# A Conformer convolution module: VectorE's tap sums in PSUM, five taps of each block on TensorE, a layer norm in a written-out order

## The chip, the cores and the metric

One Trainium2 chip, one of its cores. The metric is the device time of one execution in microseconds; lower is better. Engines by the names of the profile: PE is TensorE's matrix products (PEld its weight loads), DVE is VectorE, ACT is ScalarE, POOL is GpSimd, SP issues the DMAs.

## The reference, cut to what matters

An encoder of two layers on 256 tokens of 2048 features, in float32. The first layer's mixer is the convolution module, the second's is a gated DeltaNet; each is followed by a SwiGLU feed-forward. Only the convolution module is touched.

```python
def conformer_conv_module(h, w_pw1, b_pw1, w_dw, b_dw, ln_g, ln_b, w_pw2, b_pw2):
    u = h @ w_pw1 + b_pw1                      # 2048 -> 4096
    a, gate = jnp.split(u, 2, axis=-1)
    u = a * jax.nn.sigmoid(gate)
    u = depthwise_conv_centred(u, w_dw) + b_dw  # 31 taps along the tokens, per feature
    u = jax.nn.silu(layernorm(u, ln_g, ln_b))   # over the 2048 features of a token
    return u @ w_pw2 + b_pw2                    # 2048 -> 2048
```

## The kernel before

Activations lie with features on the 128 partitions and the 256 tokens along the free dimension, in 16 blocks of 128 features. A product is made block by block of output features (`products`): 512 KB chunks of float32 weights (`raw`, three buffers) are loaded by SP, ACT rounds half a chunk (128 x 512) to a high part `hi` (line 159), DVE subtracts to get the low part `lo` (line 160), and PE adds hi x hi, hi x lo and lo x hi in PSUM (lines 189 to 191, or 184 and 185 in the wide form). There are four buffers each for `hi` and `lo`, so these splits run at most 48 products ahead of PE.

The convolution module loops over the 16 feature blocks j. Each block has two products (`pa` and `pg`, 48 matmuls each), DVE scales them by the token's factor `rstd` (`ta`, line 325, `tg`, line 328), ACT makes the sigmoid, DVE joins them into `u` (line 330), which lies in a zero-padded tile `up`. The 31 taps of the depthwise convolution are shifted views of `up`, and they are divided among the engines:

- ACT makes tap 0 with the bias into `a` (line 336).
- For blocks 12 to 15 PE makes 8, 8, 16 and 16 taps as products with diagonal matrices (line 340), which POOL builds at the start (line 290, 48 of them).
- POOL adds 15 taps (14, 13, 6 and 5 for the last four blocks) to `a` (line 344), from products `m` that ACT makes with four buffers (line 343).
- DVE makes the rest in two running sums `b[0]` and `b[1]` in SBUF (lines 350, 352, 354); the sums are added to `a` by POOL (line 355), DVE (line 358), and for PE's part DVE (line 357).

For the layer norm, sums over the channels are made by PE with a matrix of ones (`s1` of the deviations from the first four blocks' mean `shift`, `s2` of their squares, line 302). From block 6 on the shift is subtracted within the taps (line 350), for the earlier ones by POOL (line 308). After block 15 come `dm`, `dq`, `var`, the square root on ACT and the reciprocal on DVE, and then 16 blocks of normalising: multiply by `lr` (line 386; three on DVE, thirteen on POOL), subtract `dm` (line 389, DVE), SiLU (ACT), and the split into `y` hi and lo (lines 203, 204). Then the second product `pw2` starts with three column blocks at once, all of whose `hi` and `lo` have six buffers.

Each engine's queue is in order. The order in it is set at build time by a planner, which sorts by the order of the code and by priorities (`high_priority`). The six column halves of `pw2` that fit are split before the layer norm. Four lines of the program:

```python
                w = lambda t: wdw[:, j * TAPS + t : j * TAPS + t + 1]
                x = lambda t: up[:, t : t + S]
                acc, b = new(f"a{j}", 1), (new("b0", 2), new("b1", 2))
                npe, npool = NPE.get(j, 0), NPOOL[j]
```

Of the kernel before, what the change touches and what calls it, by code (L numbers as in the profile page):

```python
# [7 lines left out]
F32 = mybir.dt.float32  # L8
# [17 lines left out]
# PSUM banks  # L26
# [3 lines left out]
LNP = 100  # L30
FIRST = 4
SHIFTED = 6
NPE = {12: 8, 13: 8, 14: 16, 15: 16}
# [4 lines left out]
# taps of the depthwise convolution that GpSimd adds, by feature block  # L38
NPOOL = [15] * 12 + [14, 13, 6, 5]

# columns of the packed per-feature parameters
# [11 lines left out]
# columns of the packed constants  # L53
# [13 lines left out]
def fv(ap, off, *dims):  # L67
    """A view of a tile by an offset and [stride, count] pairs over its free elements."""
    return bass.AP(ap.tensor, ap.offset + off, [list(ap.ap[0]), *[list(d) for d in dims]])


class Trunk:
# [20 lines left out]
    def new_h(self):  # L93
        """The residual stream on chip, in a pool of its own."""
        self.hs = ExitStack()
        hp = self.hs.enter_context(self.tc.tile_pool(name=self.nm("resid"), bufs=1))
        self.h = [hp.tile([P, S], F32, tag=f"h{k}", name=self.nm(f"h{k}")) for k in range(KD)]
# [5 lines left out]
    def load_first(self, srcs):  # L103
        """The input and the first weights, in the order in which they are needed."""
# [47 lines left out]
    def halves(self, raw, i, n, pool=None):  # L152
        """k-tiles i to i + n as a high and a low part that float32r holds exactly."""
# [9 lines left out]
    def products(self, srcs, kt, acts, wide=False, tags=("lin",), pool=None, order=None):  # L163
        """Blocks of 128 output features, k-tile by k-tile; acts: float32r tiles [P, hi | lo].

        order: of the k-tiles, within each CS of them."""
# [77 lines left out]
    def warm(self, func, after):  # L244
        """Loads a function's table on ScalarE, ahead of its use."""
# [3 lines left out]
    def rsqrt(self, src, scale, eps, then=None):  # L249
# [5 lines left out]
        nc.vector.reciprocal(r, r)  # L255
        return r

    def norm_end(self):
        """The factor is traced behind the next product, whose result is the first to need it."""
# [4 lines left out]

    def conv_module(self, next_norm):
# [3 lines left out]
        with tc.tile_pool(name="conv", bufs=1, reuse_waits="tile") as cv:  # L269
# [16 lines left out]
            diag = {}  # L286
            for j, n in NPE.items():
                for t in range(1, 1 + n):
                    g = cv.tile([P, P], F32, name=f"diag{j}_{t}")
                    nc.gpsimd.tensor_scalar(g, self.mat("ident"), wdw[:, j * TAPS + t : j * TAPS + t + 1], 0.0,  # L290
                                            op0=ALU.mult, op1=ALU.add)
                    diag[j, t] = g
# [4 lines left out]
            def add(key, t, n, last):  # L297
                """Sums over the channels, added up in PSUM."""
                if n == 0:
                    tag = "a" if key == "s1" else "b"  # L300
                    sums[key] = self.ps.tile([P, S], F32, tag=tag, bufs=PSB[tag], name=self.nm(key))
                nc.tensor.matmul(sums[key], self.mat("ones"), t, start=(n == 0), stop=last)

            def second(j):
                """The deviation from the first channels' mean, and its square's sum."""
# [6 lines left out]
                nc.scalar.activation(sq, d, AF.Square)  # L312
# [3 lines left out]
            for j in range(KD):  # L316
# [11 lines left out]
                nc.vector.tensor_tensor(tg, pg, rstd, op=ALU.mult)  # L328
                nc.scalar.activation(tg, tg, AF.Sigmoid, bias=self.p("bpw1", KD + j))
                nc.vector.scalar_tensor_tensor(u, ta, self.p("bpw1", j), tg, op0=ALU.add, op1=ALU.mult)  # L330

                w = lambda t: wdw[:, j * TAPS + t : j * TAPS + t + 1]
                x = lambda t: up[:, t : t + S]
                acc, b = new(f"a{j}", 1), (new("b0", 2), new("b1", 2))
                npe, npool = NPE.get(j, 0), NPOOL[j]
                nc.scalar.activation(acc, x(0), AF.Identity, scale=w(0), bias=self.p("bdw", j))
                if npe:
                    pt = self.ps.tile([P, S], F32, tag="b", bufs=PSB["b"], name=self.nm("taps"))
                    for t in range(1, 1 + npe):
                        nc.tensor.matmul(pt, diag[j, t], x(t), start=(t == 1), stop=(t == npe))  # L340
                for t in range(1 + npe, 1 + npe + npool):
                    m = new("m", 4)
                    nc.scalar.activation(m, x(t), AF.Copy, scale=w(t))  # L343
                    nc.gpsimd.tensor_tensor(acc, acc, m, op=ALU.add)  # L344
                t0 = 1 + npe + npool
                for t in range(t0, TAPS):
                    k = t - t0
                    r = b[k % 2]
                    if k == 1 and j >= SHIFTED:
                        nc.vector.scalar_tensor_tensor(r, x(t), w(t), shift, op0=ALU.mult, op1=ALU.subtract)  # L350
                    elif k < 2:
                        nc.vector.tensor_scalar(r, x(t), w(t), None, op0=ALU.mult)
                    else:
                        nc.vector.scalar_tensor_tensor(r, x(t), w(t), r, op0=ALU.mult, op1=ALU.add)
                (nc.vector if j == KD - 1 else nc.gpsimd).tensor_tensor(acc, acc, b[0], op=ALU.add)
                if npe:
                    nc.vector.tensor_tensor(b[1], b[1], pt, op=ALU.add)
                nc.vector.tensor_tensor(acc, acc, b[1], op=ALU.add)
# [13 lines left out]
            # mean = shift + dm: the first channels' deviations add up to nothing  # L372
# [5 lines left out]
            nc.vector.scalar_tensor_tensor(var, sums["s2"], 1.0 / D, dq, op0=ALU.mult, op1=ALU.subtract)  # L378
            lr = self.rsqrt(var, 1.0, self.c("eps5"), AF.Silu)
            # in the order in which VectorE and GpSimd get them done  # L380
            order = (0, 3, 1, 2, *range(4, KD))
            ys = [None] * KD
            for n, j in enumerate(order):
                d = ds[j]
                with tc.high_priority(LNP * (KD - n)):
                    (nc.vector if j < 3 else nc.gpsimd).tensor_tensor(d, d, lr, op=ALU.mult)
                    if j == 0:
                        nc.vector.tensor_tensor(dm, dm, lr, op=ALU.mult)
                    nc.vector.tensor_tensor(d, d, dm, op=ALU.subtract)
                    nc.scalar.activation(d, d, AF.Silu, scale=self.p("lng", j), bias=self.p("lnb", j))  # L390
                    y = cv.tile([P, 2 * S], F32R, tag=f"y{j}", name=self.nm("y"))
                    self.split(y, d)
                ys[j] = y
            self.norm_begin()
            first = self.products(self.pw2[:3], KD, ys, wide=True, tags=("lin", "lin", "g"), pool=cv, order=order)
# [44 lines left out]

    def deltanet(self, next_norm):
# [8 lines left out]
        # what the last heads leave early lies below what they need to the end  # L450
# [25 lines left out]
        # the first lie within what dn0 leaves  # L476
# [17 lines left out]
    # tiles of the DeltaNet's pool: shape, number  # L494
# [34 lines left out]
    def dn_gates(self):  # L529
        """ln(beta) and the decays' sums within a block: as a token's scalars and along the tokens."""  # L530
# [9 lines left out]
        # ln(1 + e) = 2 artanh(e / (2 + e))  # L540
# [42 lines left out]
    def short_conv(self, n):  # L583
        """Twice the SiLU of the five-tap convolution, of feature block n."""
# [92 lines left out]
    def dn_lanes(self, xd):  # L677
        """Inverses of the 32 x 32 diagonal blocks of I + X, one block in a partition."""
# [29 lines left out]
        # pairs of 4, 8 and 16  # L708
# [56 lines left out]
        # pairs of 32  # L765
# [191 lines left out]
```

## Time and profile before

| | |
|---|---|
| median of 3 runs | 3095.36 us (3088.73 to 3097.14) |
| span of the profiled execution | 3092.0 us |
| that execution's time against the median | no separate time of it is on the page; its span lies 3.4 us, or 0.1%, under the median of the runs |
| DVE, PE, POOL busy in the whole span | 2332.2, 2859.3 and 1009.9 us |
| first and last `u` of the convolution module | start 32.6 and 319.2 us |
| first product of the layer-normed data | 347.7 us |
| third column block of `pw2` complete | 364.2 us |

Busy times are unions of the instructions on an engine; an instruction's duration is longer than the distance to the next one, since neighbours overlap by some 70 ns on DVE. In rows of groups the columns are the line, the engine, the operation, output and inputs, count, then the busy time and the mean of one in ns, and then the idle time just before them with what ended it.

### The profile page before, as it was taken

What the parts mean: (1) busy time and instruction counts of PE and PEld (TensorE: products, weight loads), DVE (VectorE), ACT (ScalarE), POOL (GpSimd) and SP (SyncE); (2) the same over time, 40 slices, a digit from 0 to 9 for tenths busy, and PEclk for the clock granted to TensorE, in tenths of its full rate; (3) what the DMA queues carried; (4) which work ended last, traced back from release to release, by engine and by line L of the source; (5) the groups of instructions that cost most, each with busy time, mean ns of one, the idle gap of its engine ahead of it and who ended that gap; (6) DMA issues with size and microseconds to landing.
All of it is one profiled execution on the core that took longest, in us unless ns stands there. A gap on an engine that the chain in (4) does not pass through costs nothing. (4 is left out here: it accounts for less than half of the span.)

```text
span 3092.0 us, 50294 instructions
## 1 busy us (share of the span) xinstructions
PE 2859.3 (92%) x18122; PEld 2566.7 (83%) x18122; DVE 2332.2 (75%) x3735; ACT 1695.6 (55%) x3449; POOL 1009.9 (33%) x1047
## 2 busy tenths in 40 slices
PE   7778799999999999878888889888999999999998
PEld 6777688888888889877888888888888888888887
DVE  8999876666666667899899997985766666666555
ACT  6665555555555445654665456554545555555443
POOL 6777420000000111566667766562110000000111
PEclk9999899999999999999999999999999999999999
DMA  4333266555556665543544445456666555556664
GB/s 164 121 112 103 89 202 189 188 185 188 186 186 193 197 200 166 181 150 115 164 155 149 137 144 166 129 158 200 192 189 209 185 187 188 185 187 184 192 190 141
DMA packets 163866, 521.38 MB, mean 169 GB/s; under 512 B 18240, under 2 KB 34944, under 8 KB 163616
## 3 DMA queue, kind: packets, MB, share of 16 engines
q1 hardware_dynamic: 162320, 516.86, 52.7%
q8 instruction: 142, 2.33, 0.3%
q10 hardware_dynamic: 1296, 1.30, 0.1%
q14 instruction: 108, 0.88, 0.1%
HBM read 497.02 MB, written 21.07 MB: 168 GB/s over the span
## 5 line engine op out<-in xcount | busy, mean ns | idle before, releaser
L160 DVE TENSOR_TENSOR lo<-raw,hi 128x512 fp32r<-128x512 f32 x1764 | 1384.7, 788 | 644.6 <-ACT hi L159 638.3
L159 ACT CAST hi<-raw 128x512 fp32r<-128x512 f32 x1764 | 1085.9, 619 | 935.4 <-PE acc L185 692.8
L185 PE MATMUL acc<-xs,hi 128*128 128x512 f32 x2816 | 982.0, 398 | 0.6 <-ACT hi L159 0.6
L184 PE MATMUL acc<-xs,lo 128*128 128x256 f32 x2640 | 742.3, 281 | 0.0
L191 PE MATMUL acc<-xs,lo 128*128 128x256 f32 x2064 | 620.1, 302 | 96.4 <-DVE lo L160 95.6
L189 PE MATMUL acc<-xs,hi 128*128 128x256 f32 x2064 | 606.1, 295 | 31.1 <-ACT hi L159 18.9
L185 PEld LDWEIGHTS acc<-xs,hi 128*128 128x128 f32 x2816 | 517.7, 188 | 116.4 <-ACT hi L159 0.9
L190 PE MATMUL acc<-xs,hi 128*128 128x256 f32 x2064 | 605.2, 294 | 0.8 <-DVE xs L220 0.7
L191 PEld LDWEIGHTS acc<-xs,lo 128*128 128x128 f32 x2064 | 410.9, 200 | 128.8 <-DVE lo L160 123.0
L184 PEld LDWEIGHTS acc<-xs,lo 128*128 128x128 f32 x2640 | 499.0, 189 | 6.8
L185 PE MATMUL acc<-hs,hi 128*128 128x512 f32 x1408 | 486.8, 391 | 0.0
L189 PEld LDWEIGHTS acc<-xs,hi 128*128 128x128 f32 x2064 | 413.8, 201 | 37.1 <-ACT hi L159 21.1
L190 PEld LDWEIGHTS acc<-xs,hi 128*128 128x128 f32 x2064 | 413.9, 201 | 6.1 <-issue 4.3
L184 PE MATMUL acc<-hs,lo 128*128 128x256 f32 x1376 | 388.0, 282 | 0.0
L421 POOL TENSOR_TENSOR tg<-tg,rstd 128x256 f32<-128x256 f32 x88 | 65.0, 738 | 920.9 <-ACT tg L420 920.9
L185 PEld LDWEIGHTS acc<-hs,hi 128*128 128x128 f32 x1408 | 262.2, 188 | 53.4
L184 PEld LDWEIGHTS acc<-hs,lo 128*128 128x128 f32 x1376 | 259.9, 189 | 1.6
L230 POOL TENSOR_TENSOR sq<-h 128x256 f32<-128x256 f32 x59 | 55.0, 931 | 562.7 <-DVE h L432 383.9
L344 POOL TENSOR_TENSOR a<-a,m 128x256 f32<-128x256 f32 x218 | 196.3, 908 | 56.1 <-ACT m L343 45.8
L594 DVE SCALAR_TENSOR_TENSOR u<-t,par_sb,u 128x254 f32<-128x254 f32 (+1 forms) x256 | 178.8, 704 | 3.4 <-ACT u L590 2.2
L185 PE MATMUL acc<-ys,hi 128*128 128x512 f32 x512 | 177.8, 396 | 1.1 <-DVE ys L204 1.1
L184 PE MATMUL acc<-ys,lo 128*128 128x256 f32 x496 | 137.9, 286 | 1.8 <-ACT ys L203 1.6
(226 smaller groups left out, 3503.9 us busy)
## 6 DMA issues: line engine op xcount, KB each, us to landing
raw<-in_gu SPq DMA_DIRECT2D x352, 512.0 KB, 4.6
raw<-in_win SPq DMA_DIRECT2D x194, 512.0 KB, 3.8
raw<-in_dn SPq DMA_DIRECT2D x160, 512.0 KB, 3.6
raw<-in_pw SPq DMA_DIRECT2D x94, 512.0 KB, 3.3
raw<-in_wout SPq DMA_DIRECT2D x64, 512.0 KB, 3.7
a_d<-am SPq DMA_DIRECT2D x32, 384.0 KB, 2.7
ar<-a_d SPq DMA_DIRECT2D x32, 384.0 KB, 4.8
raw<-in_dn SPq DMA_DIRECT2D x32, 256.0 KB, 4.3
```

The costliest lines, as they stand in the source:

```text
L159: nc.scalar.copy(hi, r)
L160: nc.vector.tensor_tensor(lo, r, hi.bitcast(F32), op=ALU.subtract)
L184: nc.tensor.matmul(acc[:, S:], lo, a[:, :S], start=False, stop=False)
L185: nc.tensor.matmul(acc, hi, a, start=first, stop=last)
L189: nc.tensor.matmul(acc[:, :S], hi, a[:, :S], start=first, stop=False)
L190: nc.tensor.matmul(acc[:, :S], hi, a[:, S:], start=False, stop=False)
L191: nc.tensor.matmul(acc[:, :S], lo, a[:, :S], start=False, stop=last)
L230: (nc.vector if last else nc.gpsimd).tensor_tensor(sq, h, h, op=ALU.mult)
L344: nc.gpsimd.tensor_tensor(acc, acc, m, op=ALU.add)
L421: nc.gpsimd.tensor_tensor(tg, tg, rstd, op=ALU.mult)
L594: nc.vector.scalar_tensor_tensor(u[:, lo:hi], t[:, lo + s : hi + s], w(i), u[:, lo:hi], op0=ALU.mult, op1=ALU.add)
```

## The change

- DVE's running sums lie in PSUM (`r`, one bank of tag "b", which has two, and the one bank of "g") rather than in SBUF. The taps that were `b <- up, wdw, b` with all operands in SBUF are now `r <- up, wdw, r` with one tensor from SBUF and one from PSUM. `s2` moves to the bank "sum".
- In every block PE makes five taps (6, 6, 6 and 9 in the last four) by diagonal matrices into `r[0]`, onto which DVE then goes on adding. The matrices are made by ACT, shortly ahead of use, in 16 buffers; POOL makes none.
- POOL adds 11 taps (5 in block 15) rather than 15, and no longer adds a running sum. DVE makes 13 taps (12 in blocks 12 to 14, 15 in block 15), and adds both `r` to `a`. Tap 1 is ACT's for blocks 0 to 5, and DVE's, with the shift subtracted, after that.
- The steps of block 15 get a priority of their own (`LAST`), so that they stand ahead of later splits in the queues.
- The layer norm's factors `lr` and `ml` lie in PSUM, DVE does all 48 of its vector steps in an order written out by hand, with ACT's. The first splits of `pw2` are held behind the last square (ACT) and behind `var` (DVE).

```diff
-NPE = {12: 8, 13: 8, 14: 16, 15: 16}
+NPE = [5] * 12 + [6, 6, 6, 9]
+NPOOL = [11] * 12 + [11, 11, 11, 5]
-NPOOL = [15] * 12 + [14, 13, 6, 5]
...
-            diag = {}
-            for j, n in NPE.items():
-                for t in range(1, 1 + n):
-                    g = cv.tile([P, P], F32, name=f"diag{j}_{t}")
-                    nc.gpsimd.tensor_scalar(g, self.mat("ident"), wdw[:, j * TAPS + t : j * TAPS + t + 1], 0.0,
-                                            op0=ALU.mult, op1=ALU.add)
-                    diag[j, t] = g
...
+                with tc.high_priority(LAST if j == KD - 1 else 0):
...
+                    diags = []
+                    for t in range(2, 2 + npe):
+                        g = cv.tile([P, P], F32, tag="diag", bufs=NDIAG, name=self.nm("diag"))
+                        nc.scalar.activation(g, self.mat("ident"), AF.Copy, scale=w(t))
+                        diags.append(g)
+                    r = [self.ps.tile([P, S], F32, tag=g, bufs=PSB[g], name=self.nm("r")) for g in ("b", "g")]
+                    for n, g in enumerate(diags):
+                        nc.tensor.matmul(r[0], g, x(2 + n), start=(n == 0), stop=(n == npe - 1))
+                    if j < SHIFTED:
+                        nc.scalar.activation(r[1], x(1), AF.Copy, scale=w(1))
+                    else:
+                        nc.vector.scalar_tensor_tensor(r[1], x(1), w(1), shift, op0=ALU.mult, op1=ALU.subtract)
...
+                    rs = (own, r[1]) if own else r
+                    for n, t in enumerate(range(2 + npe + npool, TAPS)):
+                        o = rs[n % 2]
+                        if n == 0 and own:
+                            nc.vector.tensor_scalar(o, x(t), w(t), None, op0=ALU.mult)
+                        else:
+                            nc.vector.scalar_tensor_tensor(o, x(t), w(t), o, op0=ALU.mult, op1=ALU.add)
+                    if own:
+                        r.append(own)
+                    for o in r:
+                        nc.vector.tensor_tensor(acc, acc, o, op=ALU.add)
...
-            lr = self.rsqrt(var, 1.0, self.c("eps5"), AF.Silu)
+            lr, ml = (self.ps.tile([P, S], F32, tag="b", bufs=PSB["b"], name=self.nm("ln")) for _ in range(2))
+            self.rsqrt(var, 1.0, self.c("eps5"), AF.Silu, lr)
...
+            with tc.high_priority(HP), tc.manual_schedule(engines={mybir.EngineType.DVE, mybir.EngineType.Activation}):
+                nc.vector.tensor_tensor(ml, dm, lr, op=ALU.mult)
+                for n in range(KD + 4):
+                    if n < KD:
+                        nc.vector.tensor_tensor(ds[n], ds[n], lr, op=ALU.mult)
+                    if 0 <= n - 1 < KD:
+                        d = ds[n - 1]
+                        nc.vector.tensor_tensor(d, d, ml, op=ALU.subtract)
+                        nc.scalar.activation(d, d, AF.Silu, scale=self.p("lng", n - 1), bias=self.p("lnb", n - 1))
...
+            with tc.issue_after(self.sq_done.ins), tc.issue_after(known.ins):
+                first = self.products(self.pw2[:3], KD, ys, wide=True, tags=("lin", "lin", "g"), pool=cv, order=order)
```

What the planner makes of it at three places. First DVE's queue in the middle of the module, from the `u` of block 8 on. Before, where two blocks' taps stand among each other:

```order
L330 SCALAR_TENSOR_TENSOR up_222<-ta_2119,par_sb,tg_2120 128x256
L354 SCALAR_TENSOR_TENSOR b_383_1982<-up_231,wdw,b_383_1982 128x256
L354 SCALAR_TENSOR_TENSOR b_382_1981<-up_231,wdw,b_382_1981 128x256
L160 TENSOR_TENSOR lo_2374<-raw_2371,hi_2373 128x512
L354 SCALAR_TENSOR_TENSOR b_339_1767<-up_228,wdw,b_339_1767 128x256
L325 TENSOR_TENSOR ta_2333<-acc_2264,rstd_462 128x256
L160 TENSOR_TENSOR lo_2390<-raw_2371,hi_2389 128x512
```

Now, where `r_2126` is `r[1]` of block 8 and `r_2125` its `r[0]`, whose first step waits for PE's five taps:

```order
L326 SCALAR_TENSOR_TENSOR up_222<-ta_2039,par_sb,tg_2040 128x256
L347 SCALAR_TENSOR_TENSOR r_2126<-up_222,wdw,shift_1084 128x256
L161 TENSOR_TENSOR lo_2262<-raw_2259,hi_2261 128x512
L360 SCALAR_TENSOR_TENSOR r_2126<-up_222,wdw,r_2126 128x256 x4
L161 TENSOR_TENSOR lo_2278<-raw_2259,hi_2277 128x512
L360 SCALAR_TENSOR_TENSOR r_2126<-up_222,wdw,r_2126 128x256 x2
L360 SCALAR_TENSOR_TENSOR r_2125<-up_222,wdw,r_2125 128x256
L161 TENSOR_TENSOR lo_2296<-raw_2293,hi_2295 128x512
L360 SCALAR_TENSOR_TENSOR r_2125<-up_222,wdw,r_2125 128x256
L320 TENSOR_TENSOR ta_2255<-acc_2186,rstd_366 128x256
L360 SCALAR_TENSOR_TENSOR r_2125<-up_222,wdw,r_2125 128x256 x3
```

One block's taps now stand together, and up to four that build on each other follow directly. Second, ACT's queue at the start, after the squares of the input. Before, six `hi` of the second and third product go before the square root for `rstd`:

```order
L228 ACTIVATE sq_217<-h_17_93 128x256
L159 CAST hi_542<-raw_540 128x512
L159 CAST hi_558<-raw_540 128x512
L159 CAST hi_576<-raw_574 128x512
L159 CAST hi_592<-raw_574 128x512
L159 CAST hi_614<-raw_612 128x512
L159 CAST hi_630<-raw_612 128x512
L252 ACT_TABLE_LOAD
L252 ACTIVATE rstd_462<-tsum_460,cst_sb 128x256
```

Now, the end of the same stretch, in which 18 diagonal matrices (ten, and then eight) and four `hi` stand ahead of that root:

```order
L338 ACTIVATE diag_809<-cst_sb,wdw 128x128
L338 ACTIVATE diag_811<-cst_sb,wdw 128x128
L338 ACTIVATE diag_1016<-cst_sb,wdw 128x128
L160 CAST hi_482<-raw_480 128x512
L160 CAST hi_498<-raw_480 128x512
L253 ACT_TABLE_LOAD
L253 ACTIVATE rstd_366<-tsum_364,cst_sb 128x256
```

The 18 matrices are new on ACT there, and two `hi` moved behind the root. Third, DVE's queue from the end of block 15 into the layer norm. Before:

```order
L358 TENSOR_TENSOR a_716_3674<-a_716_3674,b_718_3676 128x256
L374 TENSOR_SCALAR dm_3728<-s_269_1402 128x256
L376 TENSOR_TENSOR dq_3730<-dm_3728 128x256
L378 SCALAR_TENSOR_TENSOR var_3732<-s_223_1177,dq_3730 128x256
L255 RECIPROCAL rstd_3734<-rstd_3734 128x256
L386 TENSOR_TENSOR a_76_471<-a_76_471,rstd_3734 128x256
L388 TENSOR_TENSOR dm_3728<-dm_3728,rstd_3734 128x256
L386 TENSOR_TENSOR a_119_683<-a_119_683,rstd_3734 128x256
```

Now:

```order
L384 SCALAR_TENSOR_TENSOR var_3708<-s_227_1089,dq_3706 128x256
L161 TENSOR_TENSOR lo_3828<-raw_3821,hi_3827 128x512
L161 TENSOR_TENSOR lo_3832<-raw_3823,hi_3831 128x512
L161 TENSOR_TENSOR lo_3836<-raw_3825,hi_3835 128x512
L161 TENSOR_TENSOR lo_3864<-raw_3821,hi_3863 128x512
L161 TENSOR_TENSOR lo_3868<-raw_3823,hi_3867 128x512
L161 TENSOR_TENSOR lo_3872<-raw_3825,hi_3871 128x512
L257 RECIPROCAL ln_3710<-rstd_3712 128x256
L391 TENSOR_TENSOR ln_3711<-dm_3704,ln_3710 128x256
L394 TENSOR_TENSOR a_76_375<-a_76_375,ln_3710 128x256
L394 TENSOR_TENSOR a_120_589<-a_120_589,ln_3710 128x256
L397 TENSOR_TENSOR a_76_375<-a_76_375,ln_3711 128x256
```

The six `lo` for the second product moved from among block 13's and 14's taps to between `var` and the reciprocal, and all the multiplications are on DVE. From the sixth column block of `pw2` on, the queues of DVE, ACT and PE hold the same steps in the same order as before.

More of the change, by code (lines that the diff above doesn't have):

```diff
@@ L29 @@
 OUT0 = 17
-LNP = 100
+LAST = 2500
 FIRST = 4
 SHIFTED = 6
-NPE = {12: 8, 13: 8, 14: 16, 15: 16}
+NPE = [5] * 12 + [6, 6, 6, 9]
+NPOOL = [11] * 12 + [11, 11, 11, 5]
+NDIAG = 16
 WP = 800
@@ L247, in warm, with rsqrt @@
         self.nc.scalar.activation(t, after[:, :1], func)
-    def rsqrt(self, src, scale, eps, then=None):
+    def rsqrt(self, src, scale, eps, then=None, out=None):
         nc = self.nc
@@ L254, in rsqrt @@
             self.warm(then, r)
-        nc.vector.reciprocal(r, r)
-        return r
+        out = r if out is None else out
+        nc.vector.reciprocal(out, r)
+        return out
     def norm_end(self):
@@ L299, in add @@
                 if n == 0:
-                    tag = "a" if key == "s1" else "b"
+                    tag = "a" if key == "s1" else "sum"
                     sums[key] = self.ps.tile([P, S], F32, tag=tag, bufs=PSB[tag], name=self.nm(key))
@@ L311, in second @@
                 sq = new("lsq", 2)
-                nc.scalar.activation(sq, d, AF.Square)
+                self.sq_done = nc.scalar.activation(sq, d, AF.Square)
                 add("s2", sq, j, j == KD - 1)
@@ L327, in conv_module @@
                     pg = self.linear(self.pw1[KD + j], KD, xs)
[L328 to L352, printed above, removed]
-                    else:
-                        nc.vector.scalar_tensor_tensor(r, x(t), w(t), r, op0=ALU.mult, op1=ALU.add)
@@ L355, in conv_module @@
[L355 to L358, printed above, removed]
+                with tc.high_priority(LAST if j == KD - 1 else 0):
+                    nc.vector.tensor_tensor(tg, pg, rstd, op=ALU.mult)
+                    nc.scalar.activation(tg, tg, AF.Sigmoid, bias=self.p("bpw1", KD + j))
+                    nc.vector.scalar_tensor_tensor(u, ta, self.p("bpw1", j), tg, op0=ALU.add, op1=ALU.mult)
+                    w = lambda t: wdw[:, j * TAPS + t : j * TAPS + t + 1]
+                    x = lambda t: up[:, t : t + S]
+                    acc = new(f"a{j}", 1)
+                    npe, npool = NPE[j], NPOOL[j]
+                    own = None
+                    if j == KD - 1:
+                        own = self.ps.tile([P, S], F32, tag="b", bufs=PSB["b"], name=self.nm("own"))
+                    diags = []
[8 more added lines that the diff above has]
+                        nc.scalar.activation(r[1], x(1), AF.Copy, scale=w(1))
+                    else:
+                        nc.vector.scalar_tensor_tensor(r[1], x(1), w(1), shift, op0=ALU.mult, op1=ALU.subtract)
+                    nc.scalar.activation(acc, x(0), AF.Identity, scale=w(0), bias=self.p("bdw", j))
+                    for t in range(2 + npe, 2 + npe + npool):
+                        m = new("m", 4)
+                        nc.scalar.activation(m, x(t), AF.Copy, scale=w(t))
+                        nc.gpsimd.tensor_tensor(acc, acc, m, op=ALU.add)
+                    rs = (own, r[1]) if own else r
[9 more added lines that the diff above has]
+                        nc.vector.tensor_tensor(acc, acc, o, op=ALU.add)
@@ L377, in conv_module @@
             var = new("var", 1)
-            nc.vector.scalar_tensor_tensor(var, sums["s2"], 1.0 / D, dq, op0=ALU.mult, op1=ALU.subtract)
-            lr = self.rsqrt(var, 1.0, self.c("eps5"), AF.Silu)
[L381 to L393, printed above, removed]
+            known = nc.vector.scalar_tensor_tensor(var, sums["s2"], 1.0 / D, dq, op0=ALU.mult, op1=ALU.subtract)
@@ new lines, in conv_module @@
+            lr, ml = (self.ps.tile([P, S], F32, tag="b", bufs=PSB["b"], name=self.nm("ln")) for _ in range(2))
+            self.rsqrt(var, 1.0, self.c("eps5"), AF.Silu, lr)
+            order = range(KD)
+            ys = [cv.tile([P, 2 * S], F32R, tag=f"y{j}", name=self.nm("y")) for j in order]
+            with tc.high_priority(HP), tc.manual_schedule(engines={mybir.EngineType.DVE, mybir.EngineType.Activation}):
[7 more added lines that the diff above has]
+                        nc.scalar.activation(d, d, AF.Silu, scale=self.p("lng", n - 1), bias=self.p("lnb", n - 1))
+                    if 0 <= n - 2 < KD:
+                        nc.scalar.copy(ys[n - 2][:, :S], ds[n - 2])
+                    if 0 <= n - 4 < KD:
+                        y = ys[n - 4]
+                        nc.vector.tensor_tensor(y[:, S:], ds[n - 4], y[:, :S].bitcast(F32), op=ALU.subtract)
@@ L394, in conv_module @@
             self.norm_begin()
-            first = self.products(self.pw2[:3], KD, ys, wide=True, tags=("lin", "lin", "g"), pool=cv, order=order)
+            with tc.issue_after(self.sq_done.ins), tc.issue_after(known.ins):
+                first = self.products(self.pw2[:3], KD, ys, wide=True, tags=("lin", "lin", "g"), pool=cv, order=order)
             for j in range(KD):
```

## The prediction

> **What bounds the kernel now.** I read the page's slices first, then stretches, waits, and the groups of the stretch that the change touches.
>
> ```profile
> DVE  8999876666666667899899997985766666666555
> POOL 6777420000000111566667766562110000000111
> ```
>
> A slice is 77 us: the convolution module fills the first four or five, and there DVE is full and POOL at 70%. The stretches give it from the first `u` to the last (columns: length; busy and count of PE, PEld, DVE, ACT, POOL; clock; DMA), and then all that follows the third column block of `pw2`:
>
> ```profile
> 32.60:319.20 286.60, 222.54 (x1502) 201.42 (x1500) 275.44 (x385) 175.19 (x376) 220.88 (x258) 0.95 0.34 111
> 364.00:3092.00 2728.00, 2584.22 (x16345) 2319.09 (x16343) 1995.45 (x3240) 1471.10 (x2969) 757.04 (x735) 0.98 0.56 176
> ```
>
> DVE is busy 96% of the first. The second has PE at 95%, and its queues don't change, so what the module gains or loses up to 364 us arrives at the end one to one. What does PE wait for, in the first 400 us?
>
> ```profile
> PE acc L191 <- DVE lo L160: 51.4, 57, 3.1
> SPq L149 <- DVE lo L160: 261.5, 60, 12.1
> ```
>
> It waits for weight splits, which stand among DVE's taps (columns: total, times, longest). Loads are no limit: their queue (second line) itself waits for the `lo` that frees a buffer. So DVE's work bounds the module. It consists, from first to last `u`, of:
>
> ```profile
> L354 DVE SCALAR_TENSOR_TENSOR b<-up,wdw,b 128x256 f32<-128x256 f32 x175 | 131.8, 778 | 0.0
> L160 DVE TENSOR_TENSOR lo<-raw,hi 128x512 fp32r<-128x512 f32 x119 | 113.6, 961 | 0.4 <-ACT hi L159 0.4
> L352 DVE TENSOR_SCALAR b<-up,wdw 128x256 f32<-128x256 f32 x21 | 13.5, 653 | 0.1
> L330 DVE SCALAR_TENSOR_TENSOR up<-ta,par_sb,tg 128x256 f32<-128x256 f32 x16 | 12.2, 762 | 9.9 <-ACT tg L329 9.9
> L350 DVE SCALAR_TENSOR_TENSOR b<-up,wdw,shift 128x256 f32<-128x256 f32 x9 | 8.1, 905 | 0.0
> ```
>
> With the small groups (`ta`, `tg`, the adds: 21.4 us) these make 300.6 us of durations; the busy time is 275.4, so each of the 385 overlaps its neighbour by 65 ns. A tap costs 778 ns, but not always, and some operations never vary (columns: shortest, median, longest):
>
> ```profile
> L354 DVE SCALAR_TENSOR_TENSOR b<-up,wdw,b x182: 468/948/1052, 33.9 to 327.5; 128x256 f32<-128x256 f32 x182
> L325 DVE TENSOR_TENSOR ta<-acc,rstd x16: 405/411/415, 30.7 to 303.0; 128x256 f32<-128x256 f32 x16
> L398 DVE SCALAR_TENSOR_TENSOR h<-acc,par_sb,h x16: 472/483/485, 364.2 to 440.2; 128x256 f32<-128x256 f32 x16
> 365.26 0.99 POOL L230 TENSOR_TENSOR ss<-h 128x256 f32<-128x256 f32 x1 [16.16 <-DVE h L400]
> 365.70 0.48 DVE L398 SCALAR_TENSOR_TENSOR h<-acc,par_sb,h 128x256 f32<-128x256 f32 x1
> ```
>
> The tap has two tensors from SBUF, and is 468 or about 950 ns. `ta` has one from PSUM and stays at 411 in the same crowded stretch. Line 398 is a tap's twin (a scalar by partition, one tensor from PSUM, one from SBUF) and takes 0.48 us in the middle of a POOL instruction. So DVE's two-tensor reads queue with POOL's, and a PSUM operand takes an operation out of that queue.
>
> **Part by part.** *DVE, first to last `u`.* The new order has there 192 PSUM taps, 112 `lo`, 30 adds, 29 of `ta` and `tg`, 15 `u` and 9 shifted taps. No row shows a VectorE write to PSUM; the tap's price lies between 468 (free of POOL) and 948 (as now), and I take line 398's 483, the nearest form: 92.7 us. The adds and `ta`, `tg`: 59 at 411 ns, 24.2. The `lo` lies between 0.69 free (row below) and 961:
>
> ```profile
> 10.38 0.69 DVE L160 TENSOR_TENSOR lo<-raw,hi 128x512 fp32r<-128x512 f32 x1 [0.47 <-ACT hi L159]
> L344 POOL TENSOR_TENSOR a<-a,m 128x256 f32<-128x256 f32 x210 | 189.7, 911 | 55.8 <-ACT m L343 45.8 <-DVE b L354 1.5
> ```
>
> POOL falls from 210 taps and 15 adds to 160, at some 0.8 us about 55% of the stretch rather than 77%, so I take 880 (ends 77 and 108 us): 98.6. `u` and shifted taps, a little below their rows: 17. Sum 232.5, less 65 ns for each of 387, 25.2: 207.3. But 71 now stand directly behind the one whose result they need, and such pairs don't overlap:
>
> ```profile
> 332.85 0.42 DVE L376 TENSOR_TENSOR dq<-dm 128x256 f32<-128x256 f32 x1
> 333.38 0.42 DVE L378 SCALAR_TENSOR_TENSOR var<-s,dq 128x256 f32<-128x256 f32 x1
> ```
>
> Here 0.11 us pass between them. With 0.135 us for each of the 71 (65 ns of lost overlap and 70 of gap), 9.6: DVE needs 217 us where it needed 275.
>
> *PE in that stretch.* 29 products of 48, and 78 taps where 32 stood.
>
> ```profile
> 208.00 0.28 PE L189 MATMUL acc<-xs,hi 128*128 128x256 f32 x1
> 208.12 0.28 PE L190 MATMUL acc<-xs,hi 128*128 128x256 f32 x1
> 303.17 5.88 PE L340 MATMUL taps<-up,diag 128*128 128x256 f32 x26 [2.70 <-DVE b L357]
> ```
>
> Starts are 0.12 us apart: 167 us. A tap is two rows of 0.22: 34. The channel sums, 52 rows: 11. Together 212 without a gap, and 223 at the present clock of 0.95. The other end: PE's 222.5 as it stands, restarts of its bursts included, and 92 more tap rows (there are 64): 243. So PE, which had room, now has as much to do as DVE. With no waits at all the stretch takes 223; if half of PE's 51 us of waiting stays on top of 243, 269. I take 238: DVE at 91%, PE between its two ends.
>
> *ACT, POOL, SP, banks.*
>
> ```profile
> L343 ACT ACTIVATE m<-up,wdw 128x256 f32<-128x256 f32 x213 | 100.0, 501 | 13.2 <-POOL a L344 13.1
> 23.20 1.14 ACT L159 CAST hi<-raw 128x512 fp32r<-128x512 f32 x2 [0.46 <-PE acc L190]
> 26.08 0.62 ACT L159 CAST hi<-raw 128x512 fp32r<-128x512 f32 x1 [0.67 <-PE acc L190]
> ```
>
> ACT loses four `m` a block and gains five matrices (an estimate of 0.3 us each, between nothing and the 0.5 of an `m`, which has twice the elements): with 175 of 287 us busy it has room. SP's queue doesn't change. The one bank of `r[1]` is free again with its add, which stands ahead of the next block's `u`; the bank of `s2` is idle then: both cost nothing.
>
> *The start.* POOL builds no matrices, ACT does, 18 of them ahead of the root for `rstd`.
>
> ```profile
> 20.36 26.48 POOL L290 TENSOR_SCALAR diag<-cst_sb,wdw 128x128 f32<-128x128 f32 x48 [19.21 <-DMA wdw<-in_par]
> 47.56 0.51 ACT L343 ACTIVATE m<-up,wdw 128x256 f32<-128x256 f32 x1 [6.81 <-POOL a L344]
> 49.30 0.92 DVE L330 SCALAR_TENSOR_TENSOR up<-ta,par_sb,tg 128x256 f32<-128x256 f32 x1 [7.17 <-ACT tg L329]
> ```
>
> POOL's 26 us held ACT's `m` for 6.8 us, and behind it the sigmoid, and DVE for 7.2 us; that goes, and is in the 238 already. Against it 18 x 0.3 us on ACT, less two `hi` (1.1) that moved behind and the 1.6 that ACT idled there (three waits, the first and last above): the first `u` comes at 35.3 rather than 32.6. The last: 35.3 + 238 = 273.3, 45.9 us sooner.
>
> *Block 15 and the layer norm.*
>
> ```profile
> 319.18 0.67 DVE L330 SCALAR_TENSOR_TENSOR up<-ta,par_sb,tg 128x256 f32<-128x256 f32 x1 [2.75 <-ACT tg L329]
> 331.18 0.42 DVE L358 TENSOR_TENSOR a<-a,b 128x256 f32<-128x256 f32 x1
> 335.90 1.75 DVE L255 RECIPROCAL rstd<-rstd 128x256 f32<-128x256 f32 x1 [2.09 <-ACT warm L247]
> 353.32 1.44 DVE L204 TENSOR_TENSOR y<-a,y 128x256 fp32r<-128x256 f32 x4
> 364.24 0.48 DVE L398 SCALAR_TENSOR_TENSOR h<-acc,par_sb,h 128x256 f32<-128x256 f32 x1 [2.73 <-PE acc L185]
> ```
>
> From `u` to the whole `a` are 12.4 us; now `u`, 15 taps at 0.4 and three adds make 8.2, beside PE's nine taps (4.0) and POOL's five (about 6 with their `m`): 4.2 less. From `a` to the reciprocal are 4.3; it no longer waits for the table load, but six `lo` stand ahead of it, each behind its `hi`, the last done at 3.7 + 0.7: 0.2 more. From the reciprocal's end to three column blocks 26.6; now DVE does 49 steps at 0.34 (the row of four `y`) and eight `lo` at 0.6, 21.5, and PE ends an estimated 1.7 later (six products, and the wait for the last of them): 3.4 less.
>
> Sum: -45.9 - 4.2 + 0.2 - 3.4 = -53 us, a span of 3039. The median lies 3.4 above the span: **3042 us**.
>
> [...]
>
> **Rivals.** First, two full engines wait for each other: the taps of PE need `u` from DVE, DVE's `r[0]` needs PE's taps, behind that step on DVE stand the next `lo`, for which PE waits, and ACT's `hi` stand behind `m` that wait for POOL. For it speaks that DVE and PE are within 3% of each other; against it that `lo` may run four buffers ahead. At 265 us for the stretch the time is 3069. Second, the slower side: a tap with a PSUM sum queues with POOL as before, because its scalar and its shifted tensor both come from SBUF. At 850 ns each, the middle of line 354's mean and median roughly, 192 taps cost 70 us more, the stretch 308, the time 3112; it decides above some 0.7 us a tap. The row at 365.70 speaks against it. [...] Fourth, the module's DVE falls but in-order waits eat all of it: about 3095.
>
> **How the numbers follow.** The forecast has 0.60, the first rival 0.18, the third 0.08, quicker than 3024 (all `lo` free of POOL, no waits: 223 us) 0.05, no change 0.04, the second 0.05. The range from 3024 to 3074 takes in the ends 223 and 269 of the stretch. Within 0.3% (9 us, about what this measurement can tell from no change) lies the fourth; faster has 0.91.
>
> **What would show it.** Right: the tap's line at 0.48 us with hardly any spread, DVE near 220 us between the first and the last `u`, PE's wait for `lo` far below 51, the last `u` near 273 and the first products of `y` some 10 us after the last `a` is whole (16 before: 331.6 to 347.7). Wrong: taps of 0.9 us; DVE idle behind PE's taps or ACT's `hi`; a first `u` well after 36.

## The result, and the profile after

The changed kernel takes 3014.5 us (median; 3012.9 to 3015.7) against 3094.0 us before: a ratio of 0.974, 95% interval 0.973 to 0.976. The forecast was 3042 us with a range from 3024, so the sign was right and the size was not: 79 us came instead of 53. The profiled execution took 3015.7 us with a span of 3014.0. Two rows of the page's slices show where: the crowded part is a slice shorter, DVE is no fuller than before, POOL much emptier.

```profile
DVE  8999866666666667999899998895666666666555
POOL 4763200000001113665867766451110000000011
```

The stretch from the first to the last `u`, in the columns of the prediction's stretches:

```profile
34.30:250.00 215.70, 214.64 (x1605) 207.87 (x1604) 201.99 (x389) 172.23 (x401) 151.41 (x171) 1.00 0.44 141
```

It lasts 215.7 us instead of 286.6, and the engine that fills it is PE: 214.6 us busy at a granted clock of 1.00 (0.95 before). DVE has 14 us to spare. The groups of that stretch, and below them the tap's shortest, median and longest duration:

```profile
L192 PE MATMUL acc<-xs,lo 128*128 128x256 f32 x463 | 133.4, 291 | 0.6 <-DVE lo L161 0.5
L360 DVE SCALAR_TENSOR_TENSOR r<-up,wdw,r 128x256 f32<-128x256 f32 x192 | 88.4, 482 | 3.1 <-ACT r L345 0.8
L161 DVE TENSOR_TENSOR lo<-raw,hi 128x512 fp32r<-128x512 f32 x113 | 95.7, 851 | 5.0 <-ACT hi L160 4.4
L352 POOL TENSOR_TENSOR a<-a,m 128x256 f32<-128x256 f32 x165 | 146.0, 885 | 93.0 <-ACT m L351 81.4
L360 DVE SCALAR_TENSOR_TENSOR r<-up,wdw,r x199: 472/480/491, 37.3 to 256.7; 128x256 f32<-128x256 f32 x199
```

PE waited 51.4 us for `lo`; now 0.5. A tap took 468 to 1052 ns; now 472 to 491, although POOL is busy for 70% of the stretch. Tap by tap, the trace before has 36 taps that met no POOL instruction, at 468 to 480 ns, and 146 that met one, with a median of 950; after, 191 of 199 met one and none took over 491. `lo`, whose two inputs are both in SBUF, keeps much of its price: 851 ns, 961 before.

What follows the last `u` (columns: start, duration): DVE's rows for that `u`, for the last addition to `a`, for the six `lo` and for the reciprocal, then PE's first product of `y`, and the last column block's `h`. After that, the same `h` in the kernel before.

```profile
249.97 0.48 DVE L326 SCALAR_TENSOR_TENSOR up<-ta,par_sb,tg 128x256 f32<-128x256 f32 x1 [0.58 <-ACT tg L325]
257.97 0.42 DVE L364 TENSOR_TENSOR a<-a,own 128x256 f32<-128x256 f32 x1
261.04 3.69 DVE L161 TENSOR_TENSOR lo<-raw,hi 128x512 fp32r<-128x512 f32 x6
264.65 1.75 DVE L257 RECIPROCAL ln<-rstd 128x256 f32<-128x256 f32 x1
270.23 0.79 PE L186 MATMUL acc<-y,hi 128*128 128x512 f32 x1 [9.71 <-DVE y L403]
362.88 0.48 DVE L410 SCALAR_TENSOR_TENSOR h<-acc,par_sb,h 128x256 f32<-128x256 f32 x1
```

```profile
440.25 0.48 DVE L398 SCALAR_TENSOR_TENSOR h<-acc,par_sb,h 128x256 f32<-128x256 f32 x1
```

From these rows and those of the prediction the whole difference is made up:

| piece | before | after | difference | forecast |
|---|---|---|---|---|
| start to the first `u` | 32.6 | 34.3 | +1.7 | +2.7 |
| first to last `u` | 286.6 | 215.7 | -70.9 | -48.6 |
| last `u` to whole `a` (its add's end) | 12.4 | 8.4 | -4.0 | -4.2 |
| whole `a` to the reciprocal's end | 6.1 | 8.0 | +1.9 | +0.2 |
| reciprocal's end to the last column block's `h` | 102.6 | 96.5 | -6.1 | -3.4 |
| rest of the span | | | -0.6 | 0 |
| span | 3092.0 | 3014.0 | -78.0 | -53 |

The miss is 25 us, and 22 of them lie in one row, the stretch. The experiments therefore go there.

### The profile page after: what moved, and what is told of

The parts are those of the page before. It is cut to its first block, busy times and chain, and to the rows that moved or that the text cites. A ratio compares the mean times of both kernels' runs of the same rounds, so it can differ in the third digit from the quotient of the medians.

```text
span 3014.0 us, 50376 instructions
## 1 busy us (share of the span) xinstructions
PE 2852.9 (95%) x18200; PEld 2576.3 (85%) x18200; DVE 2255.3 (75%) x3763; ACT 1698.8 (56%) x3494; POOL 912.4 (30%) x923
## 5 line engine op out<-in xcount | busy, mean ns | idle before, releaser
L161 DVE TENSOR_TENSOR lo<-raw,hi 128x512 fp32r<-128x512 f32 x1764 | 1367.3, 778 | 653.0 <-ACT hi L160 645.6
L352 POOL TENSOR_TENSOR a<-a,m 128x256 f32<-128x256 f32 x170 | 149.6, 880 | 97.6 <-ACT m L351 85.7
```

Source lines behind the costliest of these rows:

```text
L161: nc.vector.tensor_tensor(lo, r, hi.bitcast(F32), op=ALU.subtract)
```

## The experiments

Each run's time is the median of its own executions (runs 11, 12 and 13 have one each), and the kernel before had medians between 3091 and 3094 us beside them. The edits are shortened to the lines that matter. "Stretch" is always first to last `u`.

**1. The sums back in SBUF.** Only the place of DVE's running sums changes; counts, order and layer norm stay as changed.

```diff
-r = [ps.tile("b"), ps.tile("g")]            # own = ps.tile("b")
+taps = ps.tile("b"); r = [new("b0", 2), new("b1", 2)]   # own = new("b0", 2)
-scalar_tensor_tensor(o, x(t), w(t), o, ...)
+scalar_tensor_tensor(o, x(t), w(t), taps if n == 0 else o, ...)
```

> The changed kernel with DVE's running sums in SBUF; tap counts, order of steps and everything else stay (the first DVE tap reads TensorE's taps from PSUM and writes SBUF). Theory A (the place of the sums did it: a tap with a PSUM operand does not queue with POOL): the taps go from 0.48 to 0.70-0.80 us on average, DVE's busy time in the stretch first u to last u from 202 to about 250 us, PE waits for lo again for 30 us or more, stretch about 255 us, time about 3055 us. Rival B (the 48 taps taken from POOL, and the 39 more on TensorE, did it): DVE has about as many taps as before but PE and POOL share is new, the stretch stays below 230 us and the time below 3030 us.

Measured: 3056.0 us, 41 more than the changed kernel, as theory A has it. The stretch, PE's wait, and the two kinds of taps of that one line:

```profile
34.50:287.30 252.80, 225.03 (x1602) 213.63 (x1600) 247.56 (x389) 173.13 (x401) 149.44 (x171) 0.97 0.35 120
PE acc L192 <- DVE lo L161: 27.1, 18, 3.7
L363 DVE SCALAR_TENSOR_TENSOR b<-up,wdw,b x191: 468/836/1064, 36.4 to 296.3; 128x256 f32<-128x256 f32 x191
L363 DVE SCALAR_TENSOR_TENSOR b<-up,wdw,r x15: 464/469/471, 41.9 to 280.0; 128x256 f32<-128x256 f32 x15
```

The 15 taps that read PSUM stay at 464 to 471 ns; the 191 with both tensors in SBUF spread from 468 to 1064 in the same program. All 15 met a POOL instruction, as did 147 of the 191. So the place of the sum alone makes the difference, and one operand in PSUM is enough. The row shows one thing more, which matters below: PE has the same work as in the changed kernel (1602 records against 1605) but is busy 225.0 us instead of 214.6, at a clock of 0.97. With 27 us of waiting came 10 us of longer busy time.

**2. The old counts with sums in PSUM.**

```diff
-NPE = [5] * 12 + [6, 6, 6, 9];  NPOOL = [11] * 12 + [11, 11, 11, 5]
+NPE = [0] * 12 + [8, 8, 16, 16]; NPOOL = [15] * 12 + [14, 13, 6, 5]
-if n == 0 and own:               # a sum that PE doesn't start
+if n == 0 and (own or not npe):  # begins with a plain product
```

> The changed kernel with the tap counts of the kernel before: TensorE 48 taps instead of 87 (none in blocks 0 to 11), POOL 218 instead of 170, sums still in PSUM. Theory A: taps stay at 0.48 us, lo rises from 0.85 to about 0.92 us with POOL's load, DVE needs some 212 us and PE only 195 us between first and last u; stretch 212-222 us, time 3010-3025 us. Rival B (the counts did it): POOL is back at its old load, the stretch returns to 260 us or more and the time to 3055 us or more.

Measured: 3033.2 us, outside both. Taps stay at 476 ns (median), `lo` rises to 914, and DVE is busy 207.5 us, as theory A says, but the stretch is 228 us:

```profile
35.40:263.50 228.10, 205.70 (x1507) 191.69 (x1505) 207.53 (x386) 186.24 (x410) 207.25 (x219) 1.00 0.38 133
ACT m L351 <- POOL a L352: 31.6, 66, 1.1
```

DVE and POOL are both at 91%, and ACT waits 66 times for POOL to free an `m`. So the counts count too: with sums in PSUM they are worth 18 us (3033 to 3015); with the new counts the place of the sums is worth 41 (3056 to 3015). Theory A names the larger part and not the whole. These two figures, each taken beside the other half of the change, need not add up with the rest of it, and no run has the old counts and the old sums in the new order.

**3 and 4. Without POOL's additions**, in the changed kernel and in the kernel before.

```diff
-nc.gpsimd.tensor_tensor(acc, acc, m, op=ALU.add)
```

> The changed kernel without POOL's additions of its taps (these 170 products are computed by ScalarE but left out of the result). Theory C (PE bounds the stretch now, DVE has slack): lo falls from 0.85 to 0.69-0.73 us and DVE's busy time from 202 to about 187 us, yet the stretch stays at 212-216 us and the time at 3008-3015 us. Rival D (DVE and PE still wait for each other): the stretch falls with DVE by 10 us or more, time 3004 us or less.

> The kernel before without POOL's additions of its taps (218 products are left out of the result). Theory A (DVE's two-tensor SBUF operations queue with POOL's): the taps fall from 0.78 to 0.47-0.50 us, lo from 0.96 to 0.70 us, DVE's busy time from 275 to about 195 us, PE becomes the bound with about 200-215 us, time about 3020 us. If the tap's 0.78 us is its own price: DVE stays near 275 us and the time within 15 us of 3094.

Measured: 3013.1 us for the changed kernel, 3005.5 for the kernel before. The stretch and `lo` of the first, then the stretch, PE's wait, taps and `lo` of the second:

```profile
34.80:249.00 214.20, 214.06 (x1602) 207.96 (x1601) 187.19 (x388) 172.55 (x400) 4.76 (x6) 0.99 0.41 142
L161 DVE TENSOR_TENSOR lo<-raw,hi 128x512 fp32r<-128x512 f32 x113 | 78.1, 697 | 9.1 <-ACT hi L160 8.0
```

```profile
32.80:234.70 201.90, 196.51 (x1508) 190.60 (x1506) 183.06 (x387) 168.83 (x378) 34.85 (x49) 0.99 0.43 150
PE acc L191 <- DVE lo L160: 1.1, 3, 0.5
L353 DVE SCALAR_TENSOR_TENSOR b<-up,wdw,b 128x256 f32<-128x256 f32 x175 | 84.7, 515 | 0.0
L160 DVE TENSOR_TENSOR lo<-raw,hi 128x512 fp32r<-128x512 f32 x119 | 80.8, 687 | 10.2 <-ACT hi L159 9.8
```

In the changed kernel DVE gets 15 us lighter and nothing happens: PE bounds the stretch, theory C. In the kernel before, POOL's absence takes the SBUF taps from 778 to 515 ns and DVE from 275 to 183 us. Its old sums were never slow by themselves; they were slow beside POOL. It even ends below the changed kernel, and below the 3020 us expected: PE has 39 taps less in this kernel. PE makes the same products and taps as in the kernel before, yet its busy time fell from 222.5 to 196.5 us when its wait for `lo` fell from 51.4 to 1.1. The starts of its products show how: in the kernel before 172 of them came 0.2 to 0.3 us after the one ahead instead of 0.12, and PE's work broke off 71 times; here 30, and 5 times. POOL's absence by itself doesn't do that: in the changed kernel it left PE at 214 us.

**5 to 7. Two taps of blocks 0 to 14 moved: to PE from DVE, from PE to DVE, from PE to POOL.**

```diff
-NPE = [5] * 12 + [6, 6, 6, 9];  NPOOL = [11] * 12 + [11, 11, 11, 5]
+NPE = [7] * 12 + [8, 8, 8, 9]                                        # 5
+NPE = [3] * 12 + [4, 4, 4, 9]                                        # 6
+NPE = [3] * 12 + [4, 4, 4, 9]; NPOOL = [13] * 12 + [13, 13, 13, 5]   # 7
```

> The changed kernel with two taps more of blocks 0 to 14 on TensorE and two less on DVE. Theory C (PE alone bounds the stretch now): 29 taps of 0.44 us more between first and last u, 12.8 us; PE's busy time 227 us, the stretch 228 us, DVE's busy time down to 188 us with no effect; time about 3027 us. Rival D (DVE still shares the bound): the stretch falls or stays, time 3014 us or less.

> The changed kernel with two taps less of blocks 0 to 14 on TensorE and two more on DVE. PE's busy time falls to about 202 us, DVE's rises to about 214 us. If PE alone counted, the stretch would fall to 203 us and the time to 3001 us. By the prediction's failed step (two engines close to each other wait for each other) the stretch would be 225-235 us, the time 3024-3034 us with PE waiting for lo for 15 us or more. I expect between them: DVE becomes the bound at some 97%, stretch 217-223 us, time 3016-3022 us.

> The changed kernel with two taps less of blocks 0 to 14 on TensorE and two more on POOL (13). PE's busy time falls to about 202 us, POOL's rises from 151 to about 180 us, lo from 0.85 to about 0.89 us, so DVE to 206 us. Theory C: the stretch follows PE down until DVE takes over, 207-212 us, time 3005-3011 us. Rival: POOL's added load gives through lo all back, time 3014 us or more.

Measured: 3029.2, 3007.7 and 3019.0 us. The stretches in that order:

```profile
34.40:262.20 227.80, 227.36 (x1662) 219.17 (x1660) 197.82 (x358) 182.49 (x430) 145.16 (x171) 0.99 0.42 134
```

```profile
34.70:239.90 205.20, 201.44 (x1538) 195.69 (x1536) 202.23 (x414) 165.60 (x370) 165.40 (x171) 0.99 0.47 148
```

```profile
34.50:251.80 217.30, 204.75 (x1538) 195.61 (x1536) 206.35 (x389) 178.63 (x401) 187.59 (x201) 1.00 0.44 140
ACT m L351 <- POOL a L352: 17.6, 37, 1.5
```

Run 5 is theory C within a microsecond in the stretch (+12.1, 12.8 expected); only DVE's busy time fell less than expected, to 198 us instead of 188, in part because `lo` took 876 ns. Run 6 is the surprise: PE at 98% and DVE at 99% of the same 205 us, with hardly a wait between them. I had expected 217 to 223, and by the forecast's reasoning 225 to 235. DVE makes 25 steps more and is no longer busy than in the changed kernel, 12 us under my expectation: `lo` took 812 ns instead of 851, and its steps overlap by 80 ns each instead of 64 (235.3 us of durations in 202.2 of busy time). Run 7 went to the rival: neither PE nor DVE is full, and yet the stretch is 217 us.

**8. The layer norm of the kernel before**, without the new hold on `pw2`'s splits.

```diff
# in words:
-lr, ml = PSUM; ...; for n in range(KD + 4): mult (DVE); subtract (DVE); SiLU, hi (ACT); lo (DVE)
+for n, j in enumerate((0, 3, 1, 2, *range(4, KD))): mult (DVE if j < 3 else POOL); subtract; SiLU; split
-with tc.issue_after(self.sq_done.ins), tc.issue_after(known.ins):
```

> The changed kernel with the layer norm of the kernel before (13 of 16 products by GpSimd, factors in SBUF, order 0, 3, 1, 2, ...; no hold on pw2's splits). The prediction's terms for this part (reciprocal start 0.2 later, columns 3.4 sooner) say 3.2 us slower than the changed kernel; the anchors of the two traces (2.0 later, 6.0 sooner to the fourth column block) say 4 us slower: 3017-3018 us. Rival: the gain there comes from the whole order of the engines, 8 us or more slower.

Measured: 3023.8 us, 9 more than the changed kernel, so at the rival's end. By the last column block's `h` (372.2 us against 362.9) it is 9.3, in four pieces: the first `u` 0.8 later, the stretch 4.7 longer (220.4 us), last `u` to reciprocal 2.1 shorter, reciprocal to the last `h` 5.9 longer. The rows show the stretch's end on ACT and DVE, a stage of the layer norm, and the `lo` of the stretch:

```profile
252.39 2.18 ACT L161 CAST hi<-raw 128x512 fp32r<-128x512 f32 x4 [1.67 <-DMA raw<-in_pw]
253.04 2.50 DVE L162 TENSOR_TENSOR lo<-raw,hi 128x512 fp32r<-128x512 f32 x4 [2.44 <-ACT hi L161]
255.46 0.48 DVE L327 SCALAR_TENSOR_TENSOR up<-ta,par_sb,tg 128x256 f32<-128x256 f32 x1
272.86 6.13 DVE L397 TENSOR_TENSOR a<-a,dm 128x256 f32<-128x256 f32 x7
L162 DVE TENSOR_TENSOR lo<-raw,hi 128x512 fp32r<-128x512 f32 x119 | 97.3, 824 | 7.0 <-ACT hi L161 6.5
```

DVE's subtractions take 0.88 us each beside POOL's products (0.33 apart in the changed kernel), and 119 `lo` stand in the stretch rather than 113: the six of `pw2` that the hold puts behind the variance. Four of them stand right before the last `u`: ACT makes their `hi` ahead of block 15's sigmoid, after a wait for the load, and DVE, which had ended that block's `tg` at 250.6 us, comes to `u` at 255.5. In the changed kernel it is 249.4 and 250.0.

**9 and 10. The changed kernel and the one with three taps on PE, side by side.**

> The changed kernel as it is, beside the next run on the same chip, for a comparison of the two: 3012-3017 us.

> The kernel with two taps less of blocks 0 to 14 on TensorE and two more on DVE, beside the changed kernel on the same chip. If its stretch of 205 us against 216 is real, the time is 7-10 us below the changed kernel's: 3005-3009 us. If its one profile was lucky, within 3 us of it.

Measured: 3015.9 us (3013.2 to 3020.3; ratio to before 0.975, interval 0.973 to 0.976) and 3008.5 us (3003.9 to 3010.4; 0.972, 0.971 to 0.974). The executions of the two don't overlap, and the stretch repeats:

```profile
34.50:238.90 204.40, 199.67 (x1536) 193.88 (x1534) 201.91 (x413) 165.37 (x371) 165.38 (x171) 1.00 0.46 149
```

So two taps fewer on PE beat both kernels, by 7 us over the changed one.

**11 and 13. Two and three buffers of `hi` and `lo` instead of four** (`HI = 2`, `HI = 3`).

> The changed kernel with two buffers of hi and lo halves instead of four, in the whole program; only the stretch from first to last u is read. Theory E (two engines that are nearly full need not wait for each other because the halves run ahead of TensorE by up to four buffers): with two, PE waits for lo and hi for 15-40 us, its busy time grows by restarts to 220 us or more, the stretch is 235-260 us, the prediction's term. Rival F (the depth doesn't matter, PE is fed because DVE has 14 us of slack): PE's waits stay below 5 us and the stretch below 220 us.

> The changed kernel with three buffers of hi and lo halves instead of four in the whole program; only the stretch from first to last u is read (four: 215 us, two: 253 us). If four is just enough (the waits shrink with each buffer): 225-235 us, PE's wait for lo about 8 us. If three are already more than needed: 214-217 us, PE's wait for lo below 3 us.

Measured in the stretch (the whole program, which uses these buffers everywhere, takes 3335.8 and 3033.3 us): two, then three buffers.

```profile
34.10:287.10 253.00, 231.27 (x1636) 214.31 (x1634) 210.88 (x394) 178.12 (x407) 146.20 (x171) 0.99 0.39 125
PE acc L192 <- DVE lo L161: 17.3, 22, 1.3
```

```profile
35.90:255.00 219.10, 213.78 (x1589) 205.49 (x1587) 204.52 (x389) 173.98 (x402) 150.30 (x171) 1.00 0.44 139
PE acc L192 <- DVE lo L161: 3.8, 4, 1.1
```

253, 219 and 215 us with two, three and four buffers. PE's wait for `lo` is 17.3, 3.8 and 0.5 us. With two, the same engines with the same work do wait for each other (theory E), and ACT waits 59 us for PE to free a `hi`. Three come out between the two expectations, nearer to "more than needed": most of the waiting ends with the third buffer.

**12. POOL builds the diagonal matrices**, as before the change, but block by block.

```diff
-nc.scalar.activation(g, ident, AF.Copy, scale=w(t))
+nc.gpsimd.tensor_scalar(g, ident, w(t), 0.0, op0=ALU.mult, op1=ALU.add)
```

> The changed kernel with its 87 diagonal matrices built by POOL instead of ACT: 0.55 us each, of which 18 at the start. ACT is freed by 25 us in the stretch and by some 7 us at the start, POOL gets 40 us more in the stretch (151 to 190 us). The prediction's start term says the first u comes up to 2.7 us sooner (34.3 to about 32 us). POOL at 190 us is where 13 POOL taps had it (the stretch was 217 us there): I expect 216-222 us, time 3013-3020 us. Rival (POOL's matrices hold up TensorE's taps, as they stand behind POOL's additions): PE waits for diag for 10 us or more, stretch over 225 us.

Measured: one execution of 3032.0 us. The first `u` comes at 32.0, 2.3 us sooner, near the start term. The stretch is far above the 216 to 222 expected:

```profile
32.00:264.10 232.10, 220.44 (x1602) 209.31 (x1600) 204.23 (x389) 154.39 (x330) 185.59 (x242) 0.99 0.40 130
ACT m L351 <- POOL a L352: 36.5, 49, 1.7
```

The rival's length came without its cause: PE waits for no matrix. What grew is ACT's wait for POOL, as in runs 2 and 7.

**14. Run 7 with eight buffers of `m`** (which the squares at the start share).

```diff
-m = new("m", 4)
+m = new("m", 8)
```

> The run with three TensorE and 13 POOL taps, with eight buffers of m instead of four between ScalarE and POOL. Theory G (POOL's lateness reaches the others because ScalarE, in order, waits for an m buffer with the next sigmoid and hi behind it): ScalarE's wait for POOL falls from 17.6 us to below 8, the stretch from 217 to 205-210 us, the time from 3019 to 3007-3012 us. Rival H (POOL itself is late: DVE's last additions wait for its sum, and a deeper ring only moves the wait): the stretch stays at 214-220 us, the time at 3015-3022 us.

Measured: 3026.4 us, slower than run 7 by 7 us.

```profile
34.40:256.30 221.90, 205.95 (x1539) 196.82 (x1538) 208.33 (x389) 174.99 (x401) 183.35 (x201) 0.99 0.43 137
PE acc L192 <- DVE lo L161: 11.4, 16, 1.3
DVE a L364 <- POOL a L352: 7.3, 7, 2.7
```

ACT's wait for an `m` is gone, and the time with it isn't won: PE waits 11.4 us for `lo` (5.9 in run 7), and a `lo` takes 900 ns (876). So theory G falls, and rival H, which allowed 3022 us, is exceeded too. In the four runs with POOL busy for 183 us or more (2, 7, 12, 14) the stretch is 11 to 21 us longer than the busy time of its fullest engine; in run 6, with POOL at 165, it is 3. Through which wait POOL's load does this is not settled, since the wait moves when one is taken away.

## Why the prediction was right or wrong

**DVE as the bound before, and the tap freed from POOL: right.** That a tap with a PSUM operand doesn't queue with POOL was read from line 398 in the trace before. It gave 483 ns; 482 was measured, and runs 1 and 4 undo each side of it. The second rival (taps of 850 ns) is out; by the forecast's own terms it would have decided from 0.59 us a tap on, where DVE's 217 us become 238, and not from 0.7. In the changed kernel the taps with their sum in PSUM took 472 to 491 ns, 191 of 199 of them beside a POOL instruction; in run 1 those with both tensors in SBUF took 468 to 1064 ns.

**The price of PSUM: 12 ns at most.** The third rival, to which the forecast gave 0.08, was a dearer operand in PSUM. Its price came from no trace, and no run shows it: a tap that reads and writes its sum in PSUM takes 480 ns, the quickest one in SBUF 468, and one that reads PSUM and writes SBUF 469 (run 1).

**DVE's sum: 217 us forecast, 202 measured.** The durations add up to 227 instead of 232.5, since `lo`, `u` and the shifted taps came a little cheaper. The overlap of 65 ns was misread: the 300.6 us are the busy times of the groups, while their counts times their means make 306, so each operation overlapped by 79 ns; with that, the sum would have been about 212. The mean overlap is 64 ns now, since pairs that build on each other don't overlap, as forecast:

```profile
120.44 2.06 DVE L360 SCALAR_TENSOR_TENSOR r<-up,wdw,r 128x256 f32<-128x256 f32 x4
```

Four such taps start 0.53 us apart, where taps that alternate between two sums start 0.39 apart: 0.14 us a pair, for a forecast of 0.135. Most of that is in the busy time; the gaps, 3 us in the stretch, are idle time.

**The failed step: "I take 238: DVE at 91%, PE between its two ends."** PE's work was right, 212 us without a gap; 214.6 were measured, and the stretch that it fills took 215.7. But both ends were made from the kernel before in a way that carried its waits along. The lower one divided 212 by the clock of 0.95, the upper one took PE's busy time "restarts of its bursts included". Runs 1 and 4 show that both belong to the waits: the changed kernel's work costs 225.0 us with 27 us of waiting for `lo` and 214.6 with hardly any, at clocks of 0.97 and 1.00, and the old kernel's 222.5 with 51 and 196.5 with one, at 0.95 and 0.99. When DVE stopped being late, PE's busy time shrank as well. The mean clock alone doesn't give the size: 214.6 at 0.97 would be 221, and in run 11 PE is busy 231 us at 0.99.

Added to that was a remainder of mutual waiting for two engines within 3% of each other. Run 6 puts them within 1% and finds next to none of it; runs 11 and 13 show on what that hangs: with four buffers between them, and nearly so with three, the waits are gone, and with two they are not. That the buffers do it by taking up DVE's unevenness is likely but not shown. The argument "against it that `lo` may run four buffers ahead" stood in the first rival and should have set the number: 35.3 + 212 for the last `u`, with the other terms as they were a time of about 3016.

**The ends of the range.** Its lower end needed all `lo` free of POOL. They were not (851 ns), and the time fell below it all the same, because DVE no longer set it.

**The start: right in size, partly by luck**: +1.7 us for a forecast of +2.7. The matrices start 0.30 us apart, as estimated, but the trace has 16 of them ahead of the root and not 18, the root came only 0.8 us later (28.8 for 28.0), and the `hi` that moved behind it still stand ahead of the first sigmoid. Run 12 shows what the place of the matrices is worth later on: on ACT rather than on POOL they shorten the stretch by 16 us (232 to 216).

**Block 15: right** (-4.0 for -4.2). **The layer norm: twice mis-sized, in opposite directions.** The reciprocal came 1.9 us later rather than 0.2: DVE waited 1.31 us for the last channel sums and then made the six `lo` in 3.69. And from its end to the last `h` 6.1 us were won rather than 3.4: in the kernel before, the first four column blocks end one after another (`h` at 364.2, 365.7, 368.1 and 373.4 us); now `h` of the first three follow each other directly from 292.0 and the fourth starts at 296.2. I had counted to 364.2, the first of the three, as if it were the third, here and in the table of the profile before. Run 8 puts the whole part with its hold at 9 us, 4.7 of which I had not looked for: splits of `pw2` that no longer stand ahead of the last `u`.

## What to carry to other kernels

When one engine's lateness is taken away, forecast the engine behind it from its work without gaps, and ask first how many buffers lie between the two (here the stretch took 253, 219 and 215 us with two, three and four); its busy time and clock under the old waits are not its price (PE's 222.5 us at 0.95 in the kernel before were 196.5 at 0.99 in run 4). A DVE sum that was slowed beside GpSimd was freed here by moving one operand to PSUM: it cost 12 ns there, while the same operation with both tensors in SBUF took up to 1064 ns instead of 468 beside a busy GpSimd. After such a change the balance is wrong again: here, two taps of each block from TensorE back to VectorE gave another 7 us.

## What the hardware showed that I had not expected

- Two engines at 98% and 99% of a 205 us stretch, each feeding the other, with four buffers between them (run 6).
- TensorE's waits came with a longer busy time as well: 27.1 us of waiting for `lo` with 10.4 us more for the same products (run 1 against the changed kernel), and 50 us with 26 (the kernel before against run 4).
- The contention goes both ways. In the changed kernel's stretch 50 of POOL's additions met no DVE operation with two tensors from SBUF and took 725 to 754 ns; the other 121 took up to 1316. With three taps on PE, DVE's `lo` took 812 ns instead of 851, and POOL's additions became slower, from a median of 747 ns to 1012 and a busy time of 151 us to 165 (shortest, median, longest; the changed kernel, then run 6):

```profile
L352 POOL TENSOR_TENSOR a<-a,m x170: 723/747/1316, 38.0 to 255.6; 128x256 f32<-128x256 f32 x170
```

```profile
L352 POOL TENSOR_TENSOR a<-a,m x170: 722/1012/1865, 37.7 to 244.8; 128x256 f32<-128x256 f32 x170
```
